# Hybrid encoder step: 26 merge gate tiles computed first, in pairs by 7 half products, their tanh kept in DRAM

## The chip, the core and the metric

The kernel runs on one core of a Trainium2 chip. Its metric is the device time of one launch in microseconds (us). TensorE (PE) multiplies, with its weight loads shown apart (PEld); VectorE (DVE), ScalarE (ACT) and GpSimd (POOL) work on tiles of 128 partitions; SyncE (SP) issues the DMAs from one in-order queue. Each engine runs its instructions in an order fixed when the program is built.

## The reference, cut to what matters

One layer for 1024 prompt tokens and 64 sample tokens, width 1024:

```
p   = x @ w_in + b_in        # columns shared out among four token mixers, 512 wide each:
                             #   m=0 mLSTM (A), m=1 forgetting attention (B), m=2 HGRN2 (C), m=3 RG-LRU (D)
mix = sum_m sigmoid(x @ w_mg[m] + b_mg[m]) * (y_m @ w_br[m])     # w_mg[m] 1024x1024, w_br[m] 512x1024
x   = LN(alpha*x + mix @ w_out)
x   = LN(alpha*x + (gelu(causal_dwconv3(x @ w_ff_gate)) * (x @ w_ff_up)) @ w_ff_down)
```

Beside y the kernel returns the new states of the mixers.

## The kernel before

The residual stream x is kept transposed (features on partitions, 1088 tokens along the free axis) and split into a high part `xh` and a low part `xl`, both of a rounded 32-bit type, in three column chunks `CH` of 384, 384 and 320 tokens. A dense product of one output tile (128 features) takes the weights as `wh` and `wl` in the same way, and `mm3` (L250) issues three matmuls (`wh·xh`, `wh·xl`, `wl·xh`) for each of the eight 128-row pieces of the weights: 24 matmuls a chunk, 72 a tile. `dense` (L274) does the three chunks and hands each to an eviction.

`wissue` (L228) brings a 128x1024 weight block by DMA into `wr` (two buffers), rounds it to `wh` on POOL (L243) and takes `wl` as the difference on DVE (L244); it runs two blocks ahead of its use, in the order of the list `plan`. `xsplit` (L159) makes `xh` and `xl` from the rows of x: transposes on PE, `xh` on ACT, `xl` on DVE.

The merge gates are 32 tiles: for mixer m and output tile e, `gates` (L545) does the dense product with `w_mg` and evicts it as tanh (L552) into a tile `th`, since the sigmoid is (1+tanh)/2. `merge` (L556) reads a mixer's outputs y back from DRAM (`yr`), splits them into `yh` on ACT (L571) and `yl` on DVE (L572), and multiplies with `w_br`, 12 matmuls a chunk; `br` serves two output tiles with one weight block. DVE multiplies the result into `1+th` (L587), POOL adds the sum of the earlier mixers, `prev`, read from DRAM (L589), and the sum goes back to DRAM as `mx_d` (L591).

The mixers run in the order D, C, B, A. Each has its projections `P_x(u)` (dense work) and its recurrence `M_x(u)` (small matmuls with long chains over ACT and DVE between them). `weave` interleaves two generators, so that a recurrence has dense chunks on PE between its steps. `branch` (L1302) weaves `M(u-1)` with `P(u)`, and the last `M` with the gate tiles 0 to 3 of the same mixer; `merge` does gates 4 and 5 first, with the last pieces of the recurrence (`tails`) among them, then `br(0)`, `br(2)`, gates 6 and 7, `br(4)`, `br(6)`. After the mixers come `w_out`, the norm and the feed-forward part, which the diff leaves as they are.

The tile scheduler keeps what the program order and the buffers ask for and may put instructions of an engine earlier or later than they are written; `bank` gives the PSUM tiles (`pss`, `psd`, `psm`, two of each), and `slot` the 19 work tiles of 128x1088.

Of the kernel before, what the change touches and what calls it, by code (L numbers as in the profile page):

```python
# [2 lines left out]

# [6 lines left out]
F32 = mybir.dt.float32  # L10
# [9 lines left out]
P = 128  # L20
# [9 lines left out]
NSLOT = 19  # L30
FGRP = ((0, 1), (2, 3), (4, 5), (6, 7), (8, 9), (10, 11), (12, 13, 14, 15))
# [37 lines left out]
def trunk_kernel(ctx: ExitStack, tc: tile.TileContext, I, O, dbg=None):  # L69
# [6 lines left out]
    tp = ctx.enter_context(tc.tile_pool(name="tp", bufs=NSLOT))  # L76
# [3 lines left out]
    temps = [None, None]  # L80

# [26 lines left out]
    def const(shape, s, dt=F32):  # L108
        return cp.tile(list(shape), dt, tag=s, name=s)
# [16 lines left out]
    maskU = const([P, P], "maskU")  # L126
# [4 lines left out]
    trif = slot([P, P], F32, "trif")  # L131
# [51 lines left out]
    def win(c0):  # L183
        return I["w_in"][0, :, c0:c0 + P].rearrange("(k p) c -> p k c", p=P)

    def plan_cons(m):
        for kind, e in (("mg", 0), ("mg", 1), ("mg", 2), ("mg", 3), ("mg", 4), ("mg", 5), ("br", 0), ("br", 2),
                        ("mg", 6), ("mg", 7), ("br", 4), ("br", 6)):
            wide = P if kind == "mg" else 2 * P
            plan.append(((kind, m, e), I["w_" + kind][0, m, :, e * P:e * P + wide].rearrange(  # L190
                "(k p) c -> p k c", p=P), 1024 // wide))

    for u in range(4):
        for c0 in (RG_X, RG_G):
            plan.append((("in", c0 + u * P), win(c0 + u * P), 8))
    plan_cons(3)
    for u in range(4):
        for c0 in (HG_F, HG_Q, HG_I, HG_G):
            plan.append((("in", c0 + u * P), win(c0 + u * P), 8))
    plan_cons(2)  # L200
    for u in range(4):
        for c0 in (FX_K, FX_Q, FX_V):
            plan.append((("in", c0 + u * P), win(c0 + u * P), 8))
    plan_cons(1)
    for u in range(2):
        for c0 in (ML_K + u * P, ML_Q + u * P, ML_V + 2 * u * P, ML_V + 2 * u * P + P,
                   ML_O + 2 * u * P, ML_O + 2 * u * P + P):
            plan.append((("in", c0), win(c0), 8))
    plan_cons(0)
# [92 lines left out]
    pkr = slot([P, P], F32, "pkr")  # L302
    pk2 = const([P, PK2], "pk2")
    pk2r = slot([P, P], F32, "pk2r")
    xt = {}

    def xload(*tts):
        for tt in tts:
            xt[tt] = slot([P, D], F32, "xt")
            pinned(SP.dma_start(xt[tt][0:tw(tt)], xsrc(tt)))  # L310
# [59 lines left out]
    bhalf = const([P, 32], "bhalf")  # L370
    V.tensor_scalar(bhalf, pk2[:, PK_MG:PK_MG + 32], 0.5, None, OP.mult)
# [166 lines left out]
    ths = {}  # L538

# [6 lines left out]
    def gates(m, es):  # L546
        for e in es:
            th = slot([P, T], F32, "th")
            b = bhalf[:, m * 8 + e:m * 8 + e + 1]

            def ev(c, n0, n, ps, th=th, b=b):
                S.activation(th[:, n0:n0 + n], ps, AF.Tanh, bias=b, scale=0.5)  # L552
            ths[m, e] = th
            yield from dense(("mg", m, e), ev)

    def merge(m, it):  # L556
        res = []
        yh, yl = [], []
        g4 = gates(m, (4, 5))
        while tails:  # L560
            next(g4)
            flush()
# [12 lines left out]

        def br(e):
            wh, wl = wget(("br", m, e))
            for g in range(2):
                th = ths.pop((m, e + g))
# [14 lines left out]
        run(g4)  # L594
        br(0)
        br(2)
        run(gates(m, (6, 7)))
        br(4)
        br(6)
# [316 lines left out]
    def P_B(u):  # L916
# [12 lines left out]
        ks = small([P, TS], "fks", 2)  # L929
# [377 lines left out]
    first = P_D(0)  # L1307
    for c in range(1, 3):
        next(first)
        for tt in range(3 * c, 3 * c + 3):  # L1310
            xsplit(xt[tt], tt, tt != 3 * c + 1)
        next(first)
    next(first)
# [6 lines left out]
    weave(chain(fox_rows(), ml_rows()), 10, P_C(0), 12)  # L1320
    branch(2, P_C, M_C, 4, 12, 19, 1)
    merge(2, 1)
    phase("B")
    run(P_B(0))
    branch(1, P_B, M_B, 4, 9, 23, 2)
    merge(1, 2)
    phase("A")
    run(P_A(0))
    branch(0, P_A, M_A, 2, 18, 21, 3)
# [256 lines left out]
```

## Time and profile before

| | |
|---|---|
| median of 3 runs | 2186.97 us (2186.97 to 2187.04) |
| profiled execution | 2185.64 us, of which its span is 2183.9 us |
| mean granted TensorE clock | 0.996 |
| PE busy | 2133.7 us (98%), 13203 instructions |
| PEld busy | 1986.1 us (91%) |
| DVE busy | 1079.4 us (49%) |
| ACT busy | 563.4 us (26%) |
| POOL busy | 396.1 us (18%) |
| DMA | 156.76 MB, 71 GB/s over the span |

Times in the profile count from the span's start. Matmuls are pipelined: the next one starts before the one ahead of it has ended, so the duration shown with a matmul is longer than its share of PE's time. A row of the timeline gives in square brackets how long its engine sat idle before it, and what ended that. Stages by time: x is loaded and split from 0 to 41 us, D runs to about 230 us, C to about 700, B to about 1150, A to about 1500, the rest is `w_out` and the feed-forward part.

### The profile page before, as it was taken

The numbers are of one execution on the slowest core, as the hardware profiler recorded it, in microseconds if no ns is written. First come the engines' busy times: TensorE is split into PE (matmuls) and PEld (weight loads), VectorE is DVE, ScalarE is ACT, GpSimd is POOL, SyncE is SP. The second block draws the span as 40 slices with busy tenths as digits, with TensorE's granted clock in tenths as the row PEclk, the third lists the DMA queues.
The fourth block names the chain that finished last, engine by engine and source line by source line (L and its number), as shares of the span: only waits on it lengthen the run. The fifth ranks groups of instructions, "written<-read, shape, count | busy, mean of one in ns | idle before, by whom it ended". The sixth has DMA issues, their size and how long they took to land.

```text
span 2183.9 us, 31686 instructions
## 1 busy us (share of the span) xinstructions
PE 2133.7 (98%) x13203; PEld 1986.1 (91%) x13203; DVE 1079.4 (49%) x2052; ACT 563.4 (26%) x1100; POOL 396.1 (18%) x360
## 2 busy tenths in 40 slices
PE   8999999999999999999999999999999999999997
PEld 7999999888899888888999999997899999999996
DVE  4643346666433557645331245445554444445447
ACT  3653024545210234333201122310230011001111
POOL 1111001111123312210231111132410000000104
PEclk9999999999999999999999999999999999999999
DMA  5112221111143232131332111324111111111112
GB/s 149 53 59 84 97 73 36 47 44 44 46 148 122 78 100 79 51 99 50 132 131 59 59 50 54 104 99 150 49 30 39 46 42 49 44 44 39 49 58 83
DMA packets 174763, 156.76 MB, mean 72 GB/s; under 512 B 12636, under 2 KB 155304, under 8 KB 174620
## 3 DMA queue, kind: packets, MB, share of 16 engines
q1 hardware_dynamic: 174620, 154.74, 22.5%
q8 instruction: 104, 1.70, 0.3%
q14 instruction: 39, 0.32, 0.1%
HBM read 124.65 MB, written 30.06 MB: 71 GB/s over the span
## 4 chain that ended last, share of the span: by engine, by line
PE 82%; DVE 8%; issue 6%; POOL 2%; DMA 1%; ACT 1%; SPq 0%; DVEq 0%; POOLq 0%; ACTq 0%
PE psd L255 15%; PE psd L257 15%; PE psd L256 15%; PE psm L255 5%; PE psm L256 5%; PE psm L257 5%; PE pss L255 4%; PE pss L256 4%; PE pss L257 4%; DVE wl L244 2%; PE psm L987 1%; PE psm L1012 1%; POOL wh L243 1%; DVE ql L1028 1%; PE psm L1200 1%
## 5 line engine op out<-in xcount | busy, mean ns | idle before, releaser
L255 PE MATMUL psd<-xh,wh 128*128 128x384 f32 (+1 forms) x1920 | 643.5, 335 | 1.1 <-ACT xh L164 1.0
L257 PE MATMUL psd<-xh,wl 128*128 128x384 f32 (+1 forms) x1920 | 632.2, 329 | 0.0
L256 PE MATMUL psd<-xl,wh 128*128 128x384 f32 (+1 forms) x1920 | 630.8, 329 | 0.8 <-DVE xl L165 0.8
L243 POOL TENSOR_SCALAR wh<-wr 128x1024 fp32r<-128x1024 f32 x144 | 155.5, 1081 | 1269.8 <-PE psd L256 434.6
L255 PEld LDWEIGHTS psd<-xh,wh 128*128 128x128 f32 x1920 | 363.4, 189 | 7.9 <-issue 3.0
L256 PEld LDWEIGHTS psd<-xl,wh 128*128 128x128 f32 x1920 | 362.1, 189 | 2.0 <-DVE xl L165 1.0
L257 PEld LDWEIGHTS psd<-xh,wl 128*128 128x128 f32 x1920 | 362.1, 189 | 0.5 <-DVE wl L244 0.3
L244 DVE TENSOR_TENSOR wl<-wr,wh 128x1024 fp32r<-128x1024 f32 x144 | 210.5, 1465 | 253.5 <-POOL wh L243 239.6
L552 ACT ACTIVATE th<-psd,bhalf 128x384 f32<-128x384 f32 (+1 forms) x96 | 54.0, 563 | 342.5 <-PE psd L257 341.7
L255 PE MATMUL psm<-yh,wh 128*128 128x384 f32 (+1 forms) x384 | 126.2, 330 | 8.8 <-DVE th L587 8.2
L256 PE MATMUL psm<-yl,wh 128*128 128x384 f32 (+1 forms) x384 | 125.7, 327 | 0.7 <-DVE yl L572 0.7
L255 PE MATMUL psd<-x1h,wh 128*128 128x384 f32 (+1 forms) x384 | 125.5, 327 | 0.7 <-DVE x1l L175 0.7
L255 PE MATMUL psm<-x1h,wh 128*128 128x384 f32 (+1 forms) x384 | 125.3, 326 | 0.7 <-DVE cv L1446 0.7
L257 PE MATMUL psm<-yh,wl 128*128 128x384 f32 (+1 forms) x384 | 125.6, 327 | 0.0
L257 PE MATMUL psd<-x1h,wl 128*128 128x384 f32 (+1 forms) x384 | 125.3, 326 | 0.0
L257 PE MATMUL psm<-x1h,wl 128*128 128x384 f32 (+1 forms) x384 | 125.2, 326 | 0.0
L256 PE MATMUL psd<-x1l,wh 128*128 128x384 f32 (+1 forms) x384 | 125.2, 326 | 0.0
L256 PE MATMUL psm<-x1l,wh 128*128 128x384 f32 (+1 forms) x384 | 125.2, 326 | 0.0
L587 DVE SCALAR_TENSOR_TENSOR th<-th,psm 128x384 f32<-128x384 f32 (+1 forms) x96 | 50.4, 530 | 107.6 <-PE psm L257 106.4
L1423 ACT ACTIVATE gp<-psd 128x384 f32<-128x384 f32 (+1 forms) x48 | 22.0, 457 | 302.4 <-PE psd L257 302.4
L1499 DVE SCALAR_TENSOR_TENSOR acc<-acc,pss 128x1024 f32<-128x1024 f32 x54 | 65.9, 1221 | 65.5 <-PE pss L257 64.8
L1432 DVE TENSOR_SCALAR cv<-gp,pk 128x1024 f32<-128x1024 f32 (+1 forms) x32 | 21.1, 698 | 126.9 <-ACT gp L1423 126.9
(479 smaller groups left out, 3638.0 us busy)
## 6 DMA issues: line engine op xcount, KB each, us to landing
wr<-in_w_in_dram SPq DMA_DIRECT2D x48, 512.0 KB
wr<-in_w_mg_dram SPq DMA_DIRECT2D x32, 512.0 KB
mx_d<-th SPq DMA_DIRECT2D x24, 544.0 KB
prev<-mx_d SPq DMA_DIRECT2D x24, 544.0 KB
wr<-in_w_br_dram SPq DMA_DIRECT2D x16, 512.0 KB
wr<-in_w_ff_gate_dram SPq DMA_DIRECT2D x16, 512.0 KB
wr<-in_w_ff_up_dram SPq DMA_DIRECT2D x16, 512.0 KB
wr<-in_w_ff_down_dram SPq DMA_DIRECT2D x16, 512.0 KB
```

Source lines behind the costliest of these rows:

```text
L243: G.tensor_scalar(h, raw, 1.0, 1.0, OP.mult, OP.mult)
L244: V.tensor_sub(l, raw, h.bitcast(F32))
L255: PE.matmul(ps, wh, mh, start=i == 0, stop=False)
L256: PE.matmul(ps, wh, ml, start=False, stop=False)
L257: PE.matmul(ps, wl, mh, start=False, stop=i == n - 1)
L552: S.activation(th[:, n0:n0 + n], ps, AF.Tanh, bias=b, scale=0.5)
L587: V.scalar_tensor_tensor(th[:, n0:n0 + n], th[:, n0:n0 + n], 1.0, ps[:, :n], OP.add, OP.mult)
L987: PE.transpose(p3[0:sw, j, 0:w], Pt[:, s0:s0 + sw], ident[0:w, 0:w])
L1012: PE.matmul(po[64 * h:64 * h + 64, 0:P], vt[:, j, 64 * h:64 * h + 64], pair[h][:, j, :], start=j == 0, stop=j == i)
L1028: V.tensor_sub(ql[h], q32[r, t2], q1[r].bitcast(F32))
L1423: S.activation(gp[:, 2 + n0:2 + n0 + n1], ps[:, 0:n1], AF.Copy)
L1499: V.scalar_tensor_tensor(acc[tt], acc[tt], al, ps, OP.mult, OP.add)
```

## The change

Twenty-six of the 32 gate tiles (13 pairs) and two more singly are computed before D, all 28 from `x` alone, and their tanh tiles are written to DRAM (`th_d`). The four tiles (0,4) to (0,7), named in `LATE`, are computed in A. `merge` reads the tanh tiles back, and does its four weight blocks one after the other. In the pairs the columns of chunks 0 and 1 (384 each) are taken together: the two output tiles, the two halves of the 1024 input features and the two chunks make a 2x2 by 2x2 block product, and `pair` does it by 7 half products (12 matmuls of 384 columns each) instead of 8. The third chunk of 320 columns is done as before (`rest`). The half products need sums of weight blocks (`wsums`, once a pair) and sums of x (`xsums`, once). What a recurrence is woven with changes too: the last `M` of a mixer now runs beside the first `P` of the next one, `M_C(3)` beside 7 of the 9 chunks of `P_B(0)` (the other two with the tails), and the last `M_A` beside 8 of the 12 chunks of the late gates.

```diff
+LATE = ((0, 4), (0, 6))
+    slot_pool(4, True)
...
+    def wsums(ra, rb, key):
+        a11, a12, a21, a22 = ra[:, 0:4, :], ra[:, 4:8, :], rb[:, 0:4, :], rb[:, 4:8, :]
+        for j in range(2):
+            h = wide["w"].tile([P, 2, 4, P], F32R, tag="sh", name=nm("sh"))
+            l = wide["w"].tile([P, 2, 4, P], F32R, tag="sl", name=nm("sl"))
+            t = wide["w"].tile([P, 2, 4, P], F32, tag="st", name=nm("st"), bufs=1)
+            if j == 0:
+                V.tensor_tensor(t[:, 0], a21, a22, OP.add)
+                V.tensor_tensor(t[:, 1], t[:, 0], a11, OP.subtract)
+            else:
+                V.tensor_tensor(t[:, 0], a11, a21, OP.subtract)
+                V.tensor_tensor(t[:, 1], a12, a22, OP.subtract)
+                V.tensor_tensor(t[:, 1], t[:, 1], t[:, 0], OP.add)
+            G.tensor_scalar(h, t, 1.0, 1.0, OP.mult, OP.mult)
+            V.tensor_sub(l, t, h.bitcast(F32))
...
+    def xsums(k):
+        for i, c, kk in ((11, 0, k), (12, 1, k), (22, 1, k + 4), (21, 0, k + 4)):
+            f[i] = wide["p"].tile([P, 384], F32, tag="xf", name=nm("xf"), bufs=4)
+            V.tensor_tensor(f[i], xh[c][:, kk, :].bitcast(F32), xl[c][:, kk, :].bitcast(F32), OP.add)
+        V.tensor_tensor(f[11], f[12], f[11], OP.subtract)
...
+        for j, t in enumerate((f[11], f[22], f[12], f[21])):
+            S.activation(h, t, AF.Copy)
+            V.tensor_sub(l, t, h.bitcast(F32))
...
+    def pair(ka, kb, add, put):
+        product(u, a11, b11, True)
+        product(ps, a12, b21, True)
+        add(0, 0, ps, kept(u))
+        rest(wa, 0)
+        product(u, s2, t2, False)
+        product(v, s1, t1, True)
+        u2 = kept(u)
+        rest(wb, 1)
+        product(u, s3, t3, False)
+        u3 = kept(u)
+        add(1, 384, v, u3)
+        product(u, a22, t4, False)
+        put(1, 0, 384, u)
+        product(v, s4, b22, False)
+        add(0, 384, v, u2)
...
+    g0, g1 = gates(3, (0,)), gates(3, (1,))
+    for c in range(3):
+        for tt in range(3 * c, 3 * c + 3):
+            if c:
+                xsplit(xt[tt], tt, tt != 3 * c + 1)
+        next(g0)
+        next(g1)
+        if c:
+            xsums(2 * c - 2)
+            xsums(2 * c - 1)
...
     def merge(m, it):
-        g4 = gates(m, (4, 5))
-        while tails:
-            next(g4)
-            flush()
...
-                th = ths.pop((m, e + g))
+                th = slot([P, T], F32, "th")
+                SP.dma_start(th, th_d[m][e + g])
...
-        run(g4)
-        br(0)
-        br(2)
-        run(gates(m, (6, 7)))
-        br(4)
-        br(6)
...
-    def branch(m, Pg, Mg, n, nP, nM, it, ng=4):
-        for u in range(1, n):
-            weave(Mg(u - 1), nM, Pg(u), nP)
-        weave(Mg(n - 1), nM, gates(m, range(4)), 12)
...
+    for m in (3, 2, 1, 0):
+        for e in (0, 2, 4, 6):
+            if (m, e) != (3, 0) and (m, e) not in LATE:
+                run(gate_pair(m, e))
+    slot_pool(NSLOT)
+    phase("D")
     gate_rows()
...
+    weave(chain(M_D(3), fox_rows(), ml_rows()), 20, P_C(0), 12)
     merge(3, 0)
...
+    g = P_B(0)
+    weave(M_C(3), 19, islice(g, 7), 7)
+    until_flushed(g)
     merge(2, 1)
...
+    weave(M_B(3), 23, P_A(0), 18)
     merge(1, 2)
...
+    g = gates(0, (4, 5, 6, 7))
+    weave(M_A(1), 21, islice(g, 8), 8)
+    until_flushed(g)
     res = merge(0, 3)
```

The orders show two places. The first is DVE at the start, where x is split. Before, the four low parts of chunk 1 (`xl_121`) and a few small operations stand in a row, and those of chunk 2 follow them closely; `xl_121` is chunk 1, `wl_147` the second weight block:

```order
L165 TENSOR_TENSOR xl_119<-pss_197,xh_118 128x8x128
L244 TENSOR_TENSOR wl_147<-wr_144,wh_146 128x1024
L165 TENSOR_TENSOR xl_121<-pss_344,xh_120 128x8x128
L175 TENSOR_TENSOR xl_121<-psm_355,xh_120 128x4x128
L175 TENSOR_TENSOR xl_121<-psd_362,xh_120 128x4x128
L338 COPY pk<-pss_208 128x60
L369 TENSOR_SCALAR ngh<-pk 128x8
L390 TENSOR_TENSOR lb<-pk 128x4
L165 TENSOR_TENSOR xl_121<-pss_369,xh_120 128x8x128
```

So little stood between the chunks of x. In the changed kernel the low parts of chunk 2 (`xl_132`) stand among the sums. The four operations of `xl_130` (chunk 1) end at row 28 of this queue; these are its rows 51 to 62, and the one with 8x64 elements is the last part of chunk 2:

```order
L353 TENSOR_TENSOR xf_457<-xh_129,xl_130 128x384
L353 TENSOR_TENSOR xf_459<-xh_129,xl_130 128x384
L353 TENSOR_TENSOR xf_461<-xh_127,xl_128 128x384
L354 TENSOR_TENSOR xf_455<-xf_457,xf_455 128x384
L192 TENSOR_TENSOR xl_132<-psd_493,xh_131 128x4x128
L355 TENSOR_TENSOR xf_457<-xf_459,xf_457 128x384
L361 TENSOR_TENSOR xs_428<-xf_455,xs_427 128x384
L356 TENSOR_TENSOR xf_459<-xf_459,xf_455 128x384
L361 TENSOR_TENSOR xs_432<-xf_457,xs_431 128x384
L357 TENSOR_TENSOR xf_461<-xf_461,xf_459 128x384
L361 TENSOR_TENSOR xs_430<-xf_459,xs_429 128x384
L182 TENSOR_TENSOR xl_132<-pss_500,xh_131 128x8x64
```

Between the end of chunk 1 and the end of chunk 2 there are now 34 operations of DVE: 22 of 128x384 elements (`xf`, `xs`), four of 128x1024 (`wl`, `sl`, one `xl`), five weight sums `st` of 128x512 and three more parts of `xl`.

The second place is the opening of D's merge on PE. Before, the first matmul on `yh` is followed by 96 matmuls of gate tiles (`psd`, four chunks) before the second one:

```order
L256 MATMUL psd_1822<-xl_121,wh_1584 128x384
L257 MATMUL psd_1822<-xh_120,wl_1585 128x384
L255 MATMUL psm_1965<-yh_1769,wh_1792 128x384
L255 MATMUL psd_1848<-xh_122,wh_1584 128x320
L256 MATMUL psd_1848<-xl_123,wh_1584 128x320
L257 MATMUL psd_1848<-xh_122,wl_1585 128x320
```

Now it comes right after the last projection chunk `psd_4539` of C and the small transposes of the mLSTM rows (L707), and the next ones follow it:

```order
L321 MATMUL psd_4539<-xl_132,wh_4165 128x320
L322 MATMUL psd_4539<-xh_131,wl_4166 128x320
L707 MATMUL psm_4515<-ident,mlf_4374 128x4 x8
L707 MATMUL psm_4515<-ident,mlf_4374 64x4
L707 MATMUL psm_4527<-ident,mlm_4378 128x4 x8
L707 MATMUL psm_4527<-ident,mlm_4378 64x4
L320 MATMUL psm_4598<-yh_4570,wh_4301 128x384
L320 MATMUL psm_4612<-yh_4570,wh_4301 128x384
L321 MATMUL psm_4598<-yl_4571,wh_4301 128x384
L322 MATMUL psm_4598<-yh_4570,wl_4302 128x384
```

The 96 matmuls have gone to the pairs at the start, and the matmuls on `yh` and `yl` of D stand next to the chunk whose eviction ACT does ahead of `yh`.

## Rows read from the trace of the kernel before

**Rows 1.** The page: busy time, chain of waits, costliest group

```profile
PE 2133.7 (98%) x13203; PEld 1986.1 (91%) x13203; DVE 1079.4 (49%) x2052; ACT 563.4 (26%) x1100; POOL 396.1 (18%) x360
...
PE 82%; DVE 8%; issue 6%; POOL 2%; DMA 1%; ACT 1%; SPq 0%; DVEq 0%; POOLq 0%; ACTq 0%
...
L255 PE MATMUL psd<-xh,wh 128*128 128x384 f32 (+1 forms) x1920 | 643.5, 335 | 1.1 <-ACT xh L164 1.0
```

**Rows 2.** Busy time by window; granted clock, DMA share, GB/s last

```profile
0.00:50.00 50.00, 40.83 (x227) 37.35 (x228) 22.23 (x67) 15.34 (x25) 7.64 (x20) 0.93 0.54 156
...
650.00:700.00 50.00, 49.06 (x297) 48.75 (x296) 15.66 (x16) 3.38 (x6) 14.28 (x8) 1.00 0.41 136
```

**Rows 3.** Timeline of PE in a gate tile (start, duration, engine, line)

```profile
199.78 0.33 PE L255 MATMUL psd<-xh,wh 128*128 128x384 f32 x1
199.96 0.33 PE L256 MATMUL psd<-xl,wh 128*128 128x384 f32 x1
```

**Rows 4.** Timeline of ACT at the start and in C's merge

```profile
11.30 1.02 ACT L164 ACTIVATE xh<-pss 128x1024 fp32r<-128x1024 f32 x1 [0.86 <-PE pss L163]
...
603.59 1.11 ACT L571 ACTIVATE yh<-yr 128x1088 fp32r<-128x1088 f32 x1 [4.10 <-DMA yr<-y_d]
...
648.48 0.58 ACT L552 ACTIVATE th<-psd,bhalf 128x384 f32<-128x384 f32 x1 [28.51 <-PE psd L257]
652.64 0.58 ACT L552 ACTIVATE th<-psd,bhalf 128x384 f32<-128x384 f32 x1 [3.58 <-PE psd L257]
656.16 0.53 ACT L552 ACTIVATE th<-psd,bhalf 128x320 f32<-128x320 f32 x1 [2.93 <-PE psd L257]
```

**Rows 5.** Timeline of DVE at the start

```profile
12.36 1.22 DVE L165 TENSOR_TENSOR xl<-pss,xh 128x1024 fp32r<-128x1024 f32 x1
13.50 1.22 DVE L244 TENSOR_TENSOR wl<-wr,wh 128x1024 fp32r<-128x1024 f32 x1
...
22.58 0.68 DVE L175 TENSOR_TENSOR xl<-psm,xh 128x512 fp32r<-128x512 f32 x1
23.18 0.68 DVE L175 TENSOR_TENSOR xl<-psd,xh 128x512 fp32r<-128x512 f32 x1
```

**Rows 6.** Timeline of PE where chunks 0 and 2 of x begin

```profile
13.63 0.44 PE L256 MATMUL psd<-xl,wh 128*128 128x384 f32 x1 [0.75 <-DVE xl L165]
...
40.91 0.31 PE L255 MATMUL psd<-xh,wh 128*128 128x320 f32 x1
```

**Rows 7.** Timeline of PE, C's recurrence and merge, B's merge

```profile
417.21 0.30 PE L827 MATMUL psm<-ident,vT 128*64 128x128 f32 x1 [1.62 <-DVE vt L831]
...
482.83 0.30 PE L827 MATMUL psm<-ident,vT 128*64 128x128 f32 x1 [1.79 <-DVE vt L831]
...
636.28 0.41 PE L255 MATMUL psm<-yh,wh 128*128 128x320 f32 x1 [0.90 <-DVE th L587]
...
1054.35 0.62 PE L255 MATMUL psm<-yh,wh 128*128 128x384 f32 x2 [0.59 <-ACT yh L571]
1055.68 0.44 PE L256 MATMUL psm<-yl,wh 128*128 128x384 f32 x1 [0.70 <-DVE yl L572]
```

**Rows 8.** Timeline of DVE in C's and B's merge

```profile
620.43 1.23 DVE L244 TENSOR_TENSOR wl<-wr,wh 128x1024 fp32r<-128x1024 f32 x1 [7.17 <-POOL wh L243]
...
632.22 3.55 DVE L244 TENSOR_TENSOR wl<-wr,wh 128x1024 fp32r<-128x1024 f32 x1 [0.51 <-POOL wh L243]
...
1047.68 1.29 DVE L572 TENSOR_TENSOR yl<-yr,yh 128x1088 fp32r<-128x1088 f32 x1 [2.92 <-ACT yh L571]
```

**Rows 9.** Timeline of POOL in C's merge

```profile
631.13 1.05 POOL L243 TENSOR_SCALAR wh<-wr 128x1024 fp32r<-128x1024 f32 x1 [2.76 <-PE psm L256]
632.15 2.53 POOL L589 TENSOR_TENSOR th<-th,prev 128x1088 f32<-128x1088 f32 x1
```

**Rows 10.** Windows around C's merge, columns as in rows 2

```profile
612.00:616.00 4.00, 4.00 (x25) 4.00 (x24) 1.27 (x2) 0.42 (x2) 0.00 (x0) 1.00 1.05 389
...
600.00:620.00 20.00, 20.00 (x124) 19.68 (x123) 6.42 (x7) 6.81 (x9) 1.91 (x3) 1.00 0.60 219
```

More of the change, by code (lines that the diff above doesn't have):

```diff
@@ L80, in trunk_kernel @@
     temps = [None, None]
+    slots = [None, None]
+    wide = {}
     def pinned(ins, on=True):
@@ L207, in trunk_kernel @@
                    ML_O + 2 * u * P, ML_O + 2 * u * P + P):
-            plan.append((("in", c0), win(c0), 8))
-    plan_cons(0)
+            plan_in(c0)
+        if u == 0:
+            plan_br(1)
+    for m, e in LATE:
+        plan_mg(m, e)
+        plan_mg(m, e + 1)
+    plan_br(0)
     for hf in range(2):
@@ new lines, in pair, with product, rest, kept @@
+    def pair(ka, kb, add, put):
+        wissue(wpos[kb] + 2)
+        wa, wb, sums = wtiles.pop(ka), wtiles.pop(kb), wtiles.pop(("sums", kb))
+        a11, a12, a22 = [tuple(t[:, 4 * i:4 * i + 4, :] for t in w) for w, i in ((wa, 0), (wa, 1), (wb, 1))]
+        s1, s2, s3, s4 = sums
+        b11, b21, b22 = [tuple(t[c][:, 4 * i:4 * i + 4, :] for t in (xh, xl)) for c, i in ((0, 0), (0, 1), (1, 1))]
+        t1, t2, t3, t4 = [xs[j] for j in range(4)]
+        def product(ps, a, b, start, stop=True):
+            for k in range(4):
+                for i, (w, x) in enumerate(((a[0], b[0]), (a[0], b[1]), (a[1], b[0]))):
+                    PE.matmul(ps, w[:, k, :], x[:, k, :], start=start and k == 0 and i == 0, stop=k == 3 and i == 2,
+                              skip_group_check=not start)
+        def rest(w, i):
+            ps = bank("d")[:, 0:320]
+            mm3(ps, [(w[0][:, k, :], w[1][:, k, :], xh[2][:, k, :], xl[2][:, k, :]) for k in range(8)])
+            put(i, 768, 320, ps)
+        def kept(ps):
+            t = wide["p"].tile([P, 384], F32, tag="pp", name=nm("pp"), bufs=3)
+            S.activation(t, ps, AF.Copy)
+            return t
+        two = bank("s", 1024)
+        u, v = two[:, 0:384], two[:, 512:896]
+        product(u, a11, b11, True)
+        yield
+        ps = bank("d")[:, 0:384]
+        product(ps, a12, b21, True)
+        add(0, 0, ps, kept(u))
+        yield
+        rest(wa, 0)
+        yield
+        product(u, s2, t2, False)
+        yield
+        product(v, s1, t1, True)
+        u2 = kept(u)
+        yield
+        rest(wb, 1)
+        product(u, s3, t3, False)
+        u3 = kept(u)
+        yield
+        add(1, 384, v, u3)
+        product(u, a22, t4, False)
+        put(1, 0, 384, u)
+        yield
+        product(v, s4, b22, False)
+        add(0, 384, v, u2)
+        yield
@@ L308, in xload @@
         for tt in tts:
-            xt[tt] = slot([P, D], F32, "xt")
+            xt[tt] = wide["x"].tile([P, D], F32, tag=f"x{tt}", name=nm("xt")) if tt < 8 else slot([P, D], F32, "xt")
             pinned(SP.dma_start(xt[tt][0:tw(tt)], xsrc(tt)))
@@ L1299, in M_A, with until_flushed @@
         yield
-    def branch(m, Pg, Mg, n, nP, nM, it, ng=4):
-        for u in range(1, n):
-            weave(Mg(u - 1), nM, Pg(u), nP)
-        weave(Mg(n - 1), nM, gates(m, range(4)), 12)
[L1307 to L1313, printed above, removed]
+    def until_flushed(g):
+        while tails:
+            next(g)
+            flush()
+        run(g)
+    for m in (3, 2, 1, 0):
+        for e in (0, 2, 4, 6):
+            if (m, e) != (3, 0) and (m, e) not in LATE:
+                run(gate_pair(m, e))
+    slot_pool(NSLOT)
+    phase("D")
     gate_rows()
-    run(first)
-    branch(3, P_D, M_D, 4, 6, 10, 0)
+    run(P_D(0))
+    for u in range(1, 4):
+        weave(M_D(u - 1), 10, P_D(u), 6)
+    weave(chain(M_D(3), fox_rows(), ml_rows()), 20, P_C(0), 12)
     merge(3, 0)
@@ L1319, in trunk_kernel @@
     phase("C")
-    weave(chain(fox_rows(), ml_rows()), 10, P_C(0), 12)
-    branch(2, P_C, M_C, 4, 12, 19, 1)
+    for u in range(1, 4):
+        weave(M_C(u - 1), 19, P_C(u), 12)
+    g = P_B(0)
+    weave(M_C(3), 19, islice(g, 7), 7)
+    until_flushed(g)
     merge(2, 1)
     phase("B")
-    run(P_B(0))
-    branch(1, P_B, M_B, 4, 9, 23, 2)
+    for u in range(1, 4):
+        weave(M_B(u - 1), 23, P_B(u), 9)
+    weave(M_B(3), 23, P_A(0), 18)
     merge(1, 2)
     phase("A")
-    run(P_A(0))
-    branch(0, P_A, M_A, 2, 18, 21, 3)
+    weave(M_A(0), 21, P_A(1), 18)
+    g = gates(0, (4, 5, 6, 7))
+    weave(M_A(1), 21, islice(g, 8), 8)
+    until_flushed(g)
     res = merge(0, 3)
```

141 lines of the change are left out of this document (99 added, 42 removed).

## The prediction

> **What bounds the kernel now.** I read the page first. PE is busy 2133.7 of 2183.9 us, the chain of waits is PE for 82%, and no other engine comes above 49% [rows 1]. So 50 us are idle in the whole run, and a change can win only by fewer or shorter matmuls; whatever it adds elsewhere costs nothing until PE waits for it. The reader is to see next how little of the 50 us lies in steady work: a 50-us window inside C's merge has PE at 49.06, while the first window has 40.83, with a mean granted clock of 0.93 [rows 2]. The clock therefore drops in the part where x is read and split, and is full later.
>
> Then the price of a matmul. The page gives 335 ns for one [rows 1], but in the timeline the next starts 0.18 us after the one before it, which shows 0.33 [rows 3]: they overlap. The spacing of evictions gives the true share. The tanh of chunk 0 and of chunk 1 of a gate tile start 4.16 us apart, that of chunk 2 another 3.52 [rows 4], for 24 matmuls each: 173.3 ns at 384 columns and 146.7 at 320. A gate tile costs 2 x 4.16 + 3.52 = 11.84 us.
>
> **The change part by part.** The sum is made against the profiled execution, 2185.64 us.
>
> Removed: 13 pairs leave out one product of 12 matmuls of 384 columns each, 156 x 173.3 ns = **-27.0 us**. Taken at 335 ns it would be -52; that reading counts overlapped time twice.
>
> The start. Before, PE had done 96 matmuls of 384 columns, two tiles by two chunks, when chunk 2 began at 40.91 [rows 6]. Now the same 96 come first too (the two single gate tiles), so the start of chunk 2 can be compared directly. DVE sets it. The second block's `wl` stands ahead of all of chunk 0's low parts in DVE's row now. Its weights come by the second DMA, and 1.05 of rounding [rows 9] and 1.2 of `wl` [rows 5] follow before the low parts of three token tiles. I put the first run of chunk 0 at 16.9 instead of 13.63 [rows 6]. Its 48 matmuls take 8.3 us, and some 1.6 more at a clock still low, so they end near 27; transposes, `xh` (1.02 [rows 4]) and the low parts put the end of chunk 1's split at 31.5. Then come the 34 operations between the two chunks. A 512-wide one takes 0.60 from start to start and a 1024-wide one 1.14 [rows 5], so I take 0.465 for 384: 22 x 0.465 + 4 x 1.14 + 8 x 0.60 = 19.6 us, with some 1.5 for ACT, which writes the high part of each `xs` ahead of its DVE operation. Chunk 2 starts near 52.6. PE has finished chunk 1 near 41.5 and stands for about 11 us. That is 52.6 - 40.91 = 11.7 us later than before, and 1.5 more for a clock that starts low again after the wait (the first window's 0.93 is 3.5 us lost in 50 [rows 2]; I take less than half). **+13**, between 5 (most of the sums slip behind the split's own waits) and 18.
> The Trainium skill, "SBUF — State Buffer", section "Who interferes with whom", says that a DVE operation with two SBUF inputs and a GpSimd operation that reads SBUF exclude each other, whichever came first. By that rule two roundings on POOL among these 34 could add up to 2.1 us to the start; the trace agrees: the `wl` that starts at 632.22 beside the POOL addition (632.15 to 634.68) ends at 635.77, 1.1 us after that addition [rows 8, 9].
>
> In the pairs I cost the additions at nothing. A pair takes 2 x 11.84 - 2.08 = 21.6 us of PE. On DVE it has two `wl`, two `sl` at 1.14, five `st` at 0.60, three additions from PSUM: about 10 us, and up to 4.2 more where it stands beside POOL's four roundings [rows 8, 9]; ACT has some five operations of 0.5 and six tanh [rows 4]. The one tight place is `kept(u)`, which ACT must copy out before the next product may go on in the same bank; seven matmuls of the next pair are put in that gap, 1.2 us, for about 1. Had that cover gone, each pair would lose about 1 us, 13 in all.
>
> At D's start the gate rows need small weights whose DMAs stand on SP behind the stores of the last tanh tiles, which wait for ACT. Only 37 matmuls (6.4 us) cover the tanh, a store of 544 KB, two small loads and two casts. Nothing in the trace shows this chain; I take **+3**, between 0 and 6.
>
> The merge openings. Gates 4 and 5 stood on PE while ACT and DVE split y; they are gone. In D, ACT has two evictions of the last chunk (0.53 each, by the tanh of 320) before the first `yh` of 1.11 [rows 4], and `yl` takes 1.29 [rows 8]: 3.5 us with nothing else on PE. Queued behind that `yh` are three more, which the following matmuls need one by one, but those run a product ahead. In C, B and A I take 1.5 each, near the 0.59 + 0.70 that B's opening cost even with cover [rows 7]; this 1.3 is already paid. 3.5 + 4.5 - 1.3 = **+6.7**, between 1 (the split lies in the cover of the next projections) and 14 (each opening like D's).
>
> Inside the merges POOL's `prev` addition (2.53 from 632.15 [rows 9]) and the `wl` of the next weight block collide: `wl` takes 3.55 instead of 1.23 [rows 8], the multiply behind it comes late, and PE stands 0.90 at 636.28 [rows 7]. It happens where one `br` follows another directly, twice in each of the merges of C, B and A; with four in a row, three times. 3 x 0.95 = **+2.9**, between 0 and 6.
>
> The recurrences. `M_C` waits once a unit for `vt` (1.62, 1.79 [rows 7], four such), whatever dense work runs beside it. `M_C(3)` now has 9 dense chunks beside it and its tails instead of 16. I take **+1.5**, between 0 and 15, and 1.7 back for a wait of about that size at the first block of B, whose cover grows: -0.2 together.
>
> Sum: -27.0 + 13.2 + 3 + 6.7 + 2.9 - 0.2 = -1.4, so 2184.2 for the profiled execution. The median of the runs lies 1.3 above it, and the forecast for the median is 2186.97 - 1.4 = 2185.6; I say **2185**, no change that can be told (a measurement of this kernel tells 0.2%, 4.4 us).
>
> **The rivals.**
>
> First, the covered case: only the start costs. The merge openings and the gate rows find other matmuls ahead of them, as the scheduler may place projections there. -27.0 + 13.2 = -13.8: about 2173. For it speaks that PE in C's merge loses only 1 us in 50 now [rows 2]. Against it: the order shows D's `yh` matmuls directly behind the last chunk.
>
> Second, transfers bound the merges. With four `br` in a row each output tile of C and B loads `th` and `prev`, stores `mx` and needs half a weight block: 3 x 557 + 262 KB = 1.93 MB in 5.92 us, 327 GB/s. The trace shows 389 in a 4-us window with the DMA engines full, but 219 at a share of 0.60 over 20 us [rows 10]. At 219 a tile would take 8.8 us, +2.9 for 16 tiles, 47 us: 2230. The point from which it decides is a sustained rate under 327. Full engines speak for about 365 (219 / 0.60) and against it.
> The Trainium skill, "SBUF — State Buffer", section "Summary: rules for kernel authors", puts HBM traffic at about 358 GB/s; by it the merges fit with a tenth to spare, as the 365 does.
>
> Third, slower by the recurrences: `M_C(3)` and the last `M_A` run out of dense cover. A unit of `M_C` lasts 482.83 - 417.21 = 65.6 us [rows 7], of which 12 projection chunks are 47.4; the rest, 18 us, is its own matmuls and waits. With 9 chunks, 35.5 us, the unit can be no shorter than its chain over DVE and ACT. If the chain needs 65, PE stands 12 us there, and half as much in A: +17 on the sum, 2203. It decides once the chain is longer than about 54 us. Against it speaks that the waits in these rows are 1.6 to 1.8 us a unit and no more.
>
> Fourth, the naive reading: 335 ns a matmul is real PE time, -52 + 25 = -27: 2160. The 0.18 between starts speaks against it.
>
> **How the numbers follow.** The forecast (2177 to 2190 with its own spread) has 0.50: of this 0.16 is faster by over 0.2%, 0.30 within, 0.04 slower. The covered case 0.24, transfers 0.08, recurrences 0.14, the naive reading 0.04. Faster: 0.16 + 0.24 + 0.04 = 0.44; same 0.30; slower 0.04 + 0.08 + 0.14 = 0.26. The range takes the covered case with its spread and part of the third: 2168 to 2200; outside are the transfers, the naive reading and the upper part of the third.
>
> **What would show it.** PE has 156 fewer large matmuls and busy time (by spacing) 27 less. The start: chunk 2 of x begins near 52 instead of 41, PE idle about 10 us before it, the releaser DVE `xl`. In the pairs no idle of PE over 0.3 us. An idle of about 3 us ahead of D's first products with `yl`, with DVE as the releaser; three idles of about 0.9 in each of three merges. DMA windows of the merges of C and B near 330 GB/s. The prediction is wrong in its start if chunk 2 begins before 46; in its saving, if a pair is not 21.6 us; in its sum, if PE idles over 2 us in any merge tile.

## The result, and the profile after

The changed kernel takes 2237.97 us (median of 4 runs, 2234.41 to 2240.03) where the kernel before takes 2186.97: the ratio is 1.0236, with a 95% interval of 1.0218 to 1.0253. It is slower by 51 us; the forecast of 2185 with 2168 to 2200 was wrong. The profiled execution has a span of 2236.4 us, 52.5 more than before.

From the page of the changed kernel, the engines (before's are in [rows 1]) and TensorE's granted clock in 40 slices of the span.

```profile
PE 2143.8 (96%) x13047; PEld 1976.9 (88%) x13047; DVE 1201.6 (54%) x2230; ACT 589.9 (26%) x1142; POOL 424.8 (19%) x386
...
PEclk8999999998999999999999999989999999999999
```

PE's busy time has gone up by 10 us although 156 large matmuls are gone. The clock row has 8 in three slices, where before had 9 throughout.

Stages in the changed kernel (columns as in [rows 2]; window, then length, busy time of PE, PEld, DVE, ACT, POOL, granted clock, DMA share, GB/s): the start, the opening of D's merge, C's merge, and the end of A's recurrence with A's merge.

```profile
0.00:60.00 60.00, 38.41 (x205) 35.93 (x206) 37.18 (x74) 18.32 (x29) 10.12 (x21) 0.86 0.38 120
510.00:550.00 40.00, 31.15 (x159) 27.37 (x158) 22.14 (x41) 9.02 (x14) 2.09 (x2) 0.74 0.53 180
840.00:900.00 60.00, 54.66 (x307) 51.55 (x308) 31.47 (x40) 3.37 (x5) 30.23 (x24) 0.94 0.79 270
1460.00:1550.00 90.00, 74.44 (x376) 68.28 (x376) 54.56 (x86) 18.02 (x42) 30.95 (x18) 0.91 0.56 191
```

The same stages before, where a merge still had its gate tiles in it and is longer for that:

```profile
0.00:60.00 60.00, 50.83 (x291) 46.98 (x292) 29.62 (x77) 20.34 (x32) 10.65 (x22) 0.94 0.49 137
180.00:240.00 60.00, 60.00 (x367) 60.00 (x365) 20.27 (x24) 9.19 (x13) 7.80 (x6) 1.00 0.32 111
590.00:700.00 110.00, 108.16 (x651) 106.22 (x650) 41.45 (x48) 12.72 (x23) 31.38 (x20) 1.00 0.40 138
1420.00:1500.00 80.00, 73.87 (x427) 70.63 (x427) 48.23 (x67) 13.47 (x37) 30.45 (x17) 1.00 0.33 112
```

PE's idle time, length less busy, was 9.2 us at the start and is 21.6; around D's merge it was 0 and is 8.9 in 40 us at a granted clock of 0.74; in C's merge 1.8 and 5.3; at A's end 6.1 and 15.6 at 0.91. Over the whole span idle time has gone from 50.2 to 92.6 us. Summed over 10-us windows, PE's busy time multiplied by what the clock lacks of 1.00 has gone from 3.3 to 26.2 us. So 42 us are new waits and, by this estimate, 23 us are work done at half speed after waits; 27 us of matmuls are gone, which makes 38 of the 52.5. Of the other 14 us, 7 lie in the pairs, in waits too short to show as idle (below); the last 7 are not located.

The opening of D's merge, timeline of PE. In brackets, the idle time and what ended it:

```profile
520.32 0.67 PE L707 MATMUL psm<-ident,mli 4*128 4x4 f32 x9 [2.51 <-DVE mli L677]
...
524.19 1.04 PE L707 MATMUL psm<-ident,mlf 4*128 4x4 f32 x9 [2.09 <-issue]
...
528.57 0.52 PE L321 MATMUL psm<-yl,wh 128*128 128x384 f32 x1
528.89 0.52 PE L322 MATMUL psm<-yh,wl 128*128 128x384 f32 x1
...
535.54 0.69 PE L320 MATMUL psm<-yh,wh 128*128 128x384 f32 x1 [3.12 <-ACT yh L739]
```

The small transposes of the mLSTM rows (L707) wait 2.51 and 2.09, the products of the third y 3.12. Between the waits matmuls of 384 columns start 0.32 us apart (528.57, 528.89), nearly twice the spacing of [rows 3]: that is the lower level of the clock, 1.2 GHz (0.54 granted from 520 to 530). SyncE's queue over the same time:

```profile
516.21 0.36 SPq L734 DMA_DIRECT2D yr<-y_d  x1
521.87 0.25 SPq L679 DMA_DIRECT2D mr_d<-mlF  x1
...
524.19 0.24 SPq L690 DMA_DIRECT2D me_d<-gm  x1
524.48 0.35 SPq L734 DMA_DIRECT2D yr<-y_d  x1
...
528.87 0.38 SPq L271 DMA_DIRECT2D wr<-in_w_in_dram  x1
529.35 0.53 SPq L734 DMA_DIRECT2D yr<-y_d  x1
```

The first read of y is issued at 516.21, the second at 524.48 and the third at 529.35. The second stands behind stores of the mLSTM rows (521.87, 524.19) and the third also behind a weight load of the next stage (528.87), each of which waits for its own data or buffer. In A it is the same, with the store of a tanh tile and a weight load ahead of the third read (SyncE, and then PE):

```profile
1475.57 0.32 SPq L490 DMA_DIRECT2D th_d<-th  x1
1477.75 0.38 SPq L271 DMA_DIRECT2D wr<-in_w_out_dram  x1
1478.23 0.42 SPq L734 DMA_DIRECT2D yr<-y_d  x1
```

```profile
1484.04 0.69 PE L320 MATMUL psm<-yh,wh 128*128 128x384 f32 x1 [3.65 <-ACT yh L739]
```

### The profile page after: what moved, and what is told of

It is laid out like the page before. It is cut to its first block, busy times and chain, and to the rows that moved or that the text cites. A ratio compares the mean times of both kernels' runs of the same rounds, so it can differ in the third digit from the quotient of the medians.

```text
span 2236.4 us, 31882 instructions
## 1 busy us (share of the span) xinstructions
PE 2143.8 (96%) x13047; PEld 1976.9 (88%) x13047; DVE 1201.6 (54%) x2230; ACT 589.9 (26%) x1142; POOL 424.8 (19%) x386
## 5 line engine op out<-in xcount | busy, mean ns | idle before, releaser
L320 PE MATMUL psd<-xh,wh 128*128 128x384 f32 (+1 forms) x1504 | 506.6, 337 | 8.6 <-DVE xl L192 7.7
L321 PE MATMUL psd<-xl,wh 128*128 128x384 f32 (+1 forms) x1504 | 494.9, 329 | 3.0 <-DVE xl L182 3.0
L322 PE MATMUL psd<-xh,wl 128*128 128x384 f32 (+1 forms) x1504 | 495.6, 330 | 0.0
L320 PEld LDWEIGHTS psd<-xh,wh 128*128 128x128 f32 x1504 | 287.2, 191 | 15.9 <-issue 11.9
L321 PEld LDWEIGHTS psd<-xl,wh 128*128 128x128 f32 x1504 | 285.9, 190 | 4.9 <-DVE xl L182 3.6
L322 PEld LDWEIGHTS psd<-xh,wl 128*128 128x128 f32 x1504 | 286.0, 190 | 0.5
L320 PE MATMUL psm<-yh,wh 128*128 128x384 f32 (+1 forms) x384 | 132.4, 349 | 22.0 <-DVE th L755 13.2
L321 PE MATMUL psm<-yl,wh 128*128 128x384 f32 (+1 forms) x384 | 131.6, 343 | 4.6 <-DVE yl L740 4.6
L322 PE MATMUL psm<-yh,wl 128*128 128x384 f32 (+1 forms) x384 | 130.2, 339 | 0.0
L320 PEld LDWEIGHTS psm<-yh,wh 128*128 128x128 f32 x384 | 75.1, 197 | 29.3 <-DVE th L755 18.3
L755 DVE SCALAR_TENSOR_TENSOR th<-th,psm 128x384 f32<-128x384 f32 (+1 forms) x96 | 50.2, 529 | 89.7 <-PE psm L322 84.5
```

Source lines behind the costliest of these rows:

```text
L320: PE.matmul(ps, wh, mh, start=i == 0, stop=False)
L321: PE.matmul(ps, wh, ml, start=False, stop=False)
L322: PE.matmul(ps, wl, mh, start=False, stop=i == n - 1)
L755: V.scalar_tensor_tensor(th[:, n0:n0 + n], th[:, n0:n0 + n], 1.0, ps[:, :n], OP.add, OP.mult)
```

## The experiments

Ratios are to the kernel before on the same chip, where it took 2183.7 to 2185.4 us. A gain over the changed kernel is given as a range, by the ratios and by the times, where the two differ; the intervals of the two ratios leave such a difference open by some 5 us.

**The move alone (e1, e14).** e1 computes the 26 tiles in the same place by plain products; e14 is e1 without the sums of x.

```diff
-                plan_pair(plan_mg, (m, e), (m, e + 1))
+                plan_mg(m, e)
+                plan_mg(m, e + 1)
...
-                run(gate_pair(m, e))
+                run(gates(m, (e, e + 1)))
```

```diff
-        if c:
-            xsums(2 * c - 2)
-            xsums(2 * c - 1)
```

> The 26 tiles are computed in the same place by plain dense products of 8 halves; the sums of weights are gone, the sums of x stay. Theory A (the trace of the changed kernel shows a pair every 22.14 us, so a pair gives back 23.68 - 22.14 = 1.54 us): slower than the changed kernel by 13 x 1.54 = 20 us, less some 5 us for the weight sums that no longer stand before chunk 2 on DVE, about 2253. Rival B (a pair costs the 21.6 us of its matmuls, as predicted): 27 us less 5, about 2260. Rival C (the sums slow other stages too): not slower than 2240.

> The kernel of e1 without the sums of x: what is left of the change is the move alone, 28 gate tiles ahead of D as plain products, their tanh through DRAM, and the new weaves; no pair and no sum. Theory A (the move costs far more than the pairs give back; the sums add only at the start): about 6 us under e1, 2241, still 55 us over the kernel before. Rival B (what is lost comes with the sums and the pairs): near the kernel before, 2195 or less.

e1: 2247.01 us, ratio 1.0287 (1.0271 to 1.0303). e14: 2240.36, ratio 1.0257 (1.0240 to 1.0274). The kernel e14 multiplies exactly what the kernel before multiplies, 32 plain tiles, with no sum and no pair, and is 57 us slower. So the loss is in the move and the weaves that came with it. The sums of x add 0.3% (6.6 us), and the pairs with their sums of weights give back 9 to 11 us: not 27. For e1 none of the three expectations came true: it is 6 us under theory A. Its 20 us for the pairs do stand in the trace (two plain tiles in a row take 23.7 us, a pair 22.14), but the sums of weights cost more than the 5 us put for them: in the first 60 us PE is idle for 15.2 us in e1 at a granted clock of 0.94, and for 21.6 at 0.86 in the changed kernel. In e14 the start has 10.2 us idle, near the 9.2 of before, and the opening of D's merge is as bad as in the changed kernel:

```profile
0.00:60.00 60.00, 49.85 (x288) 47.26 (x289) 22.34 (x65) 18.09 (x27) 7.74 (x20) 1.00 0.50 158
520.00:530.00 10.00, 5.81 (x40) 5.01 (x38) 10.00 (x25) 2.75 (x5) 2.05 (x1) 0.79 0.19 58
530.00:540.00 10.00, 6.43 (x21) 4.33 (x21) 4.51 (x9) 2.08 (x4) 0.00 (x0) 0.50 0.70 231
```

PE idles 4.2 and 3.6 us in the two 10-us windows, at 0.79 and 0.50 of the clock. Over its whole span e14 has 29.4 us more idle time than the kernel before and 18.6 us more for the clock; some 9 of its 57 us are in neither, though it has no pair; where they lie is not known.

**The start (e2).** All of x is split ahead of the sums; two tiles more are plain, to cover them (12 pairs).

```diff
-        if c:
-            xsums(2 * c - 2)
-            xsums(2 * c - 1)
     run(g0, g1)
+    for k in range(4):
+        xsums(k)
+    run(gates(3, (2, 3)))
...
```

> All of x is split before the sums of x are taken, and the tiles (3,2) and (3,3) are done plainly beside these sums; 12 pairs instead of 13. Theory A (the wait for chunk 2 behind the sums, 9.6 us idle and about 3 us of half clock, is time lost): faster than the changed kernel by 12 less 1.5 for the pair, about 2228. Rival B (the sums are late anyway and the first pair waits for them as long): about 2238 to 2240.

2224.62 us, ratio 1.0182 (1.0165 to 1.0199). Theory A holds: 12 to 13 us faster than the changed kernel, with a pair fewer. There PE waited for chunk 2, and DVE ended the two longest waits with the parts of `xl` that stand among the sums (PE, then DVE):

```profile
43.14 0.41 PE L320 MATMUL psd<-xh,wh 128*128 128x320 f32 x1 [0.64 <-ACT xh L181]
50.47 0.60 PE L320 MATMUL psd<-xh,wh 128*128 128x320 f32 x1 [6.91 <-DVE xl L192]
53.78 0.63 PE L321 MATMUL psd<-xl,wh 128*128 128x320 f32 x1 [2.71 <-DVE xl L182]
```

```profile
49.63 0.69 DVE L192 TENSOR_TENSOR xl<-psd,xh 128x512 fp32r<-128x512 f32 x1
...
53.05 0.68 DVE L182 TENSOR_TENSOR xl<-pss,xh 128x512 fp32r<-128x512 f32 x1
```

With the split first in the program the second tile's product on chunk 2 starts 7.2 us sooner (43.25), and the wait for the last part of `xl` is gone:

```profile
42.60 0.41 PE L323 MATMUL psd<-xh,wh 128*128 128x320 f32 x1 [0.64 <-ACT xh L181]
43.25 0.38 PE L323 MATMUL psd<-xh,wh 128*128 128x320 f32 x1 [0.24 <-DVE xl L192]
```

**Cover at the openings (e3).** Two gate tiles of each mixer stay behind, to stand on PE while y is read and split (9 pairs).

```diff
+COVER = ((0, 2), (1, 6), (2, 6), (3, 6))
...
+        e = COVER[m][1]
+        run(gates(m, (e, e + 1)))
         for e in range(0, 8, 2):
```

> Two gate tiles of each mixer are computed plainly at the opening of its merge (9 pairs instead of 13; 8 more plain tiles as cover). Theory A (the merge openings lose, idle and half clock together, 16 us in D, 6 in C, 4 in B, 14 in A because nothing stands beside the reading and splitting of y): about 30 of these 40 us come back, less 4 x 1.54 = 6: about 2214. Rival B (the loss is in the transfers of the tanh tiles inside the merges): 2238 + 6 = 2244, with the waits moved into the merges.

2214.46 us, ratio 1.0137 (1.0122 to 1.0152): 22 to 23.5 us faster than the changed kernel, as theory A said, although four pairs fewer are made. With 1.5 us for each of these pairs, cover brings 28 to 30 us. Rival B fell: with the same sizes of transfer in the merges the waits went. What stays in D is the wait for the mLSTM rows and part of that for the third read of y; in the 40 us from 425 PE is idle for 4.8 us at a granted clock of 0.87, which is some 9 us lost:

```profile
434.24 0.56 PE L710 MATMUL psm<-ident,mli 4*128 4x4 f32 x4 [2.61 <-DVE mli L680]
...
452.35 0.62 PE L323 MATMUL psm<-yh,wh 128*128 128x384 f32 x2 [1.52 <-ACT yh L742]
```

**The mLSTM rows (e4).** Moved to the recurrence before.

```diff
-        weave(M_D(u - 1), 10, P_D(u), 6)
-    weave(chain(M_D(3), fox_rows(), ml_rows()), 20, P_C(0), 12)
+        weave(chain(M_D(u - 1), ml_rows()) if u == 3 else M_D(u - 1), 16 if u == 3 else 10, P_D(u), 6)
+    weave(chain(M_D(3), fox_rows()), 15, P_C(0), 12)
```

> Only the row operations of the mLSTM (ml_rows) move, from D's last recurrence to the one before it. Theory A (D's opening is late because these rows, on DVE and on SP's queue, stand ahead of the reads of y): some 10 of the 16 us lost there come back, about 2228. Rival B (what is late is the split of y alone, which nothing covers): 3 us at most, 2235 or more.

2243.78 us, ratio 1.0272 (1.0257 to 1.0287): no gain, and rather a loss. Theory A fell, and not to B alone. The rows take their wait along: their transposes stand on PE close behind the operations of DVE that make the rows (6.30 at 479.79, and 1.63 at 482.49); and D's opening still waits for the third read of y (542.84), with a weight load ahead of it on SyncE:

```profile
479.79 1.07 PE L707 MATMUL psm<-ident,mli 4*128 4x4 f32 x9 [6.30 <-DVE mli L677]
...
542.84 0.69 PE L320 MATMUL psm<-yh,wh 128*128 128x384 f32 x1 [3.32 <-ACT yh L739]
```

**The queue of the reads (e7).** The reads of y are issued by ScalarE.

```diff
-                SP.dma_start(y, y_d[m][j])
+                S.dma_start(y, y_d[m][j])
```

> The reads of y in the merges are issued by ScalarE instead of SyncE, the rest is as in the changed kernel. Theory A (the third read of y stands on SyncE's queue behind weight loads and small stores that wait: PE idles 3.1 us for it in D and 3.7 in A, and the clock is at half for some 20 matmuls after each): about 10 us faster, 2228. Rival B (the reads come late because y itself was written late, or because ScalarE now waits at them): 2236 or more.

2232.00 us, ratio 1.0217 (1.0200 to 1.0234): between the two theories, and the interval overlaps the changed kernel's. A's third read cost 0.93 instead of 3.65, D's 1.70 instead of 3.12, but the reads now wait in ScalarE's order behind evictions. From 1460 to 1550 the idle time fell from 15.6 to 12.6 us; from 510 to 550 it did not (8.9 before the edit, 9.8 with it), since the transposes of the mLSTM rows wait 4.50 there now. So a gain by the queue is seen in A's waits, and is not shown in the time.

**The shared port (e8, e12).** VectorE adds `prev` in the place of GpSimd, in the changed kernel (e8) and, with the same edit, in the kernel before (e12).

```diff
-                    G.tensor_tensor(th, th, prev, OP.add)
+                    V.tensor_tensor(th, th, prev, OP.add)
```

> The addition of prev in the merges is done by VectorE instead of GpSimd, the rest is as in the changed kernel. Theory A (each weight block after the first meets this addition on the port that both engines use, and PE loses 0.92 idle and 0.3 more each time, nine times): about 11 us faster, 2227. Rival B (VectorE has no room for 24 additions of 1.2 us between the products' evictions, and PE waits for those instead): 2238 or more.

> The kernel before with one edit: the addition of prev on VectorE instead of GpSimd. If the collisions on the shared port cost there what they cost in the changed kernel (about 1.2 us each, six in the merges of C, B and A and some of those at the end of A), 7 to 9 us faster than before: 2177. If the mid-merge gate tiles hide them, 2184.

e8: 2224.39 us, ratio 1.0184 (1.0169 to 1.0199), as theory A said. e12: 2178.18 us, ratio 0.9970 (0.9958 to 0.9981), near the 2177 expected if the collisions cost there as well; it is the only version here that beats both kernels; its PE, DVE, ACT and POOL times:

```profile
PE 2132.9 (98%) x13203; PEld 1986.2 (91%) x13203; DVE 1082.2 (50%) x2076; ACT 563.3 (26%) x1100; POOL 335.3 (15%) x336
```

In the changed kernel each weight block of C's merge behind the first met the addition (DVE, POOL, PE):

```profile
860.37 3.57 DVE L284 TENSOR_TENSOR wl<-wr,wh 128x1024 fp32r<-128x1024 f32 x1 [0.51 <-POOL wh L283]
...
860.30 2.56 POOL L757 TENSOR_TENSOR th<-th,prev 128x1088 f32<-128x1088 f32 x1
...
864.46 0.41 PE L320 MATMUL psm<-yh,wh 128*128 128x320 f32 x1 [0.93 <-DVE th L755]
```

In e8 the same `wl` takes 1.2 us, and the weight blocks follow each other 11.84 us apart, which is the matmuls' own time, instead of 13.09:

```profile
862.04 1.22 DVE L284 TENSOR_TENSOR wl<-wr,wh 128x1024 fp32r<-128x1024 f32 x1
...
873.88 1.21 DVE L284 TENSOR_TENSOR wl<-wr,wh 128x1024 fp32r<-128x1024 f32 x1
```

The edit is worth 11 to 13.6 us in the changed kernel and 6.2 before; the difference, 5 to 7 us, is hardly more than what the intervals leave open. The traces show what four weight blocks in a row cost against two and two: PE has nine such idles of 0.83 to 0.99 us, three in each merge of C, B and A, where before it had six of 0.90 to 1.14; in e8 all nine are gone. At 1.25 us a block, the three more are some 4 us.

In "SBUF — State Buffer", section "Who interferes with whom", the Trainium skill says that a VectorE operation with two SBUF inputs and a GpSimd operation that reads SBUF exclude each other, and that the order of issue decides which one is blocked; the trace agrees (the addition ends at 860.30 + 2.56, and `wl`, which started behind it, 1.1 us after).

One wait of the merges is of another kind. In B the first multiplication waits for a tanh tile from DRAM, whose read stands on SyncE's queue behind a weight load (DVE, and then PE); e8 still has this wait, and in e3 it is gone:

```profile
1245.14 1.02 DVE L755 SCALAR_TENSOR_TENSOR th<-th,psm 128x384 f32<-128x384 f32 x2 [3.33 <-DMA th<-th_d]
...
1245.75 0.41 PE L320 MATMUL psm<-yh,wh 128*128 128x320 f32 x1 [2.92 <-DVE th L755]
```

**The order within a pair (e10).**

```diff
-        rest(wb, 1)
         product(u, s3, t3, False)
         u3 = kept(u)
         yield
+        rest(wb, 1)
         add(1, 384, v, u3)
```

> In a pair the 24 matmuls of the second 320-column rest are put behind the product s3*t3 instead of ahead of it, so that they cover the copy of the running sum out of PSUM; the same matmuls otherwise. Theory A (a pair takes 22.14 us instead of the 21.6 of its matmuls because PE waits 0.27 us longer than a matmul's spacing at the two products behind that copy, too short to show as idle): 13 x 0.54 = 7 us faster, 2231. Rival B (the 0.54 us lie elsewhere in the pair or move to another product): 2236 or more.

2234.19 us, ratio 1.0227 (1.0212 to 1.0243), the same as the changed kernel within the intervals. In the changed kernel two pairs start 22.14 us apart. Twice in a pair a product starts 0.30 or 0.31 us behind the matmul ahead of it, and its second matmul another 0.28 later, where 0.17 is the rule, without any idle time shown:

```profile
130.84 0.33 PE L376 MATMUL psd<-xh,wh 128*128 128x384 f32 x1
...
147.28 0.34 PE L376 MATMUL pss<-xh,wh 128*128 128x384 f32 x1
147.58 0.61 PE L376 MATMUL pss<-xs,wh 128*128 128x384 f32 x2
...
150.31 0.34 PE L376 MATMUL pss<-xl,wh 128*128 128x384 f32 x1
150.62 0.44 PE L376 MATMUL pss<-xh,sh 128*128 128x384 f32 x1
150.90 0.34 PE L376 MATMUL pss<-xl,sh 128*128 128x384 f32 x1
...
152.98 0.33 PE L376 MATMUL psd<-xh,wh 128*128 128x384 f32 x1
```

DVE and ACT at the same two places:

```profile
146.96 0.56 DVE L501 TENSOR_TENSOR th<-pss,pp 128x384 f32<-128x384 f32 x1 [1.85 <-ACT pp L386]
...
149.99 0.58 ACT L498 ACTIVATE th<-pss,bhalf 128x384 f32<-128x384 f32 x1 [1.81 <-PE pss L376]
```

The product a22*t4, which adds to `u`, starts at 147.58, as soon as DVE has read `v` for its addition (147.52); the product s4*b22, which adds to `v`, starts at 150.62, as soon as ACT has read `u` for the tanh (150.57). So these two waits do not end with the copy of `u`, as theory A had it, but with a reader of the other half: `u` and `v` are two halves of one PSUM tile (`two = bank("s", 1024)`). That is read from the kernel and from what ended the waits, the same in all 13 pairs; a version with two tiles was not run.

In e10 the pair takes 22.29 us: the first wait has moved to s3*t3, which the second rest no longer covers, and ends there with the copy of `u`; it is now long enough to show. The second wait stays as it was.

```profile
140.75 0.59 PE L376 MATMUL pss<-xs,sh 128*128 128x384 f32 x2 [0.15 <-ACT pp L386]
```

So rival B holds; where the pair loses its 0.54 us is shown, a cure is not.

**Together (e6, e9, e11).** e6 is e2 with e3; e9 adds e8's edit. e11 also puts D's merge, the fox and mLSTM rows and the last recurrences of C and A back as they were woven before (7 pairs, 18 other tiles plain up front or as cover):

```diff
+    g = gates(3, (4, 5, 6, 7))
+    weave(M_D(3), 10, islice(g, 9), 9)
+    merge(3, 0, g)
...
+    weave(chain(fox_rows(), ml_rows()), 10, P_C(0), 12)
...
+    weave(M_C(3), 19, P_B(0), 9)
...
```

> The two edits e2 and e3 together (x split ahead of the sums; two plain gate tiles as cover at each merge opening; 8 pairs). If the two losses are separate pieces of PE's time, their gains add: 2238 - 13.4 - 23.5 = 2201. If both came from one thing (the clock, say), less than 10 us beyond the better of the two: 2207 or more.

> The edits e2, e3 and e8 together in the changed kernel, 8 pairs. If the three losses add: 2202.3 - 13.6 = 2189. If the addition matters only beside the changed openings: 2200.

> Put together from the runs: x split ahead of the sums; D's merge, the fox and mLSTM rows and the last recurrences of C and A woven as before, with plain gate tiles as cover (7 pairs, 18 plain tiles); the addition of prev on VectorE. If the losses are the pieces named, 2202 - 13 (addition) - 8 (rows) - 5 (cover of M_C(3) and M_A(1)) + 1.5 (a pair less) = 2178, 0.3% under the kernel before. If gains have been counted twice, 2184 or more.

e6: 2202.33 us, ratio 1.0086 (1.0071 to 1.0102). e9: 2188.86, ratio 1.0024 (1.0015 to 1.0033). The three losses are separate pieces and add within 2 us. e11: 2185.65, ratio 1.0004 (0.9996 to 1.0013), a miss by 8 us, and within what was given for gains counted twice. Against e9 it gains 3 us where 11 were expected. The new weaves bring waits of their own, at the first block of C (L1003, after `vt`) and at A's opening; whether these are all of the miss was not tested:

```profile
520.56 0.27 PE L1003 MATMUL psm<-ident,vT 128*64 128x128 f32 x1 [3.38 <-DVE vt L1007]
...
1440.91 0.69 PE L328 MATMUL psm<-yh,wh 128*128 128x384 f32 x1 [2.61 <-ACT yh L752]
```

With seven pairs and most of the losses named here taken back, e11 stands 7 us behind e12, which has no pair at all.

## Why the prediction was wrong, point by point

- **The step that failed is the term of the merge openings**, put at +6.7 with 1 to 14. In its place the runs showed 28 to 30 us that cover takes back (e3), and some 9 more that stay at D's opening even with cover. Three things were missing. I let one read of y and its split stand for the opening ("those run a product ahead"), while the reads come one by one off SyncE's queue, behind weight loads and stores that wait: 13 us lie between the first and the third in D. I did not count the mLSTM rows there at all, which the change had put just ahead of D's opening. And the clock, for which I had 1.6 and 1.5 us at the start and nothing elsewhere, costs 23 us more than before by the windows, 7 of them in D's opening alone. In the stages of the merges the clock had been full before, where PE hardly stood; [rows 2] showed the price of waits (0.93 in the first window), and I used it for the start only. The Trainium skill, "TensorE: Matmul & The Clock Gate", section "HAM oscillation — how this bites in real kernels", tells of a kernel whose short bursts of matmuls stand between waits, and says that each burst starts again at the slow clock; the windows of D's opening agree (0.54 and 0.50 granted).
- **The saving** of 27.0 us was mis-sized: a pair takes 22.14 us, not 21.6 (7 us in 13 pairs), and e1 against the changed kernel shows a gain of 9 to 11 us, sums of weights and all. The seven matmuls (146.24 to 147.45) did cover the copy for `kept`, which ended at 146.93, but not DVE's addition behind it; the wait for the tanh of `u` I did not have.
- **The start**, +13: 15 us by the windows (12.4 idle, the rest by the clock), and e2 gave 12 to 13 back. One matmul of chunk 2 ran at 43.14, before the 46 that was to refute the start; the next ones waited until 50.47 and 53.78, where I had 52.6, with the releaser named. So the mechanism and the size were right, and that sign was badly chosen.
- **The collisions**, +2.9: right in mechanism, place and number, three more than before. Each costs more than the 0.95 that I counted: an idle of 0.93 is a step of 1.27 between two matmuls, where 0.17 is the rule, and a weight block with a collision took 13.09 us instead of 11.84. So it is some 4 us.
- **Gate rows**, +3: PE idles 2.1 us there. Near. **The recurrences**, -0.2: the waits at `vt` are 6.4 us in sum, where they were 6.7. The longest, 3.12, stands in `M_C(3)`, and the clock was at 0.87 and 0.79 in the two 10-us windows around it, some 3 us that I had left out. The third rival had the place, at less than half of the 12 us that it gave C.
- **What is left.** As measured, these terms give 41 to 43 of the 52.5 us: -20 for the pairs, 15 for the start, 2 for the gate rows, 37 to 39 for the openings, 4 and 3. Some 10 are left; the short waits that are not located (7) would be most of them.
- **The rivals.** Transfers as the bound of the merges came near in time (2230) and is wrong: in e8, from 850 to 895, PE was busy for 44.99 of 45 us with DMA at 300 GB/s, so there the blocks followed each other without a wait for data as soon as the port was free. The one wait of a merge for a tanh tile cost PE 2.92 us, at the opening of B's. The covered case assumed cover, and the order had shown that there was none; with cover the kernel is faster, but e3 stands at 2214 and e9 at 2189, and not at the 2173 of that case.

Two more of the prediction's own signs of being wrong came true: a pair was not 21.6 us, and PE idled over 2 us in the merges of D and A (3.12 and 3.65).

How the 16 us of D's opening (8.9 idle, 7 by the clock) divide between the rows, the queue and the missing cover was not settled: e4 and e7 each moved a part of the wait elsewhere.

## What to carry to other kernels

Work that depends on nothing can be worth more as cover than in a cheaper form: here two gate tiles in a pair save 1.5 us, and the same two at an opening saved some 7, as a mean over the four. Before moving such work away, list for the place that it leaves every wait that ends there now, the queue of each DMA on which it hangs, and half speed for the burst behind each wait. To test a clever change, first time the move without the cleverness.

## What the runs showed of the hardware

A wait shorter than a matmul's overlap shows no idle time: the steps of 0.31 and 0.28 us in the pairs, against 0.17, are 0.25 us each time, which only the starts show. Moving 24 additions of 2.5 us from GpSimd to VectorE cost VectorE almost nothing (1079.4 us busy before, 1082.2 in e12): the additions took it 34.2 us, and its 144 `wl` 27.3 us less than before, since those beside an addition fell from 3.55 to 1.2 us.
